# Another split of attention's steps over the blocks, and a quarter of the longest heads' differences on VectorE

## The chip, the cores and the metric

The kernel runs on one core of one Trainium2 chip. The metric is device time in microseconds. The kernel before was timed three times: 2462.47 us in the median, 2457.55 the lowest, 2462.65 the highest. Engines are named as in the profile: PE (TensorE), PEld (its weight loads), DVE (VectorE), ACT (ScalarE), POOL (GpSimd) and SP (SyncE, which only issues transfers).

## The reference

One layer on x of 2048 x 1024 in float32. A shared RMS norm and one projection feed three mixers: a gated convolution of width 3, a gated convolution of width 31 with a layer norm, and eight heads of stick-breaking attention. Their outputs are joined, projected by w_out and added to x; a squared-ReLU MLP of width 4096 and a last RMS norm follow. The attention is the part around the change:

```python
z = jnp.einsum("bhqd,bhkd->bhqk", qb, kb).astype(jnp.float32) * scale
mask = s_idx < t_idx
log_beta = jax.nn.log_sigmoid(z)
log_1m = jnp.where(mask, log_beta - z, 0.0)
suffix = lax.cumsum(log_1m, axis=3, reverse=True) - log_1m
a = jnp.where(mask, jnp.exp(log_beta + suffix), 0.0)
outs.append(jnp.einsum("bhqk,bhkd->bhqd", a.astype(v.dtype), vb))
```

The weight of a key is sigmoid(z) times the product of sigmoid(-z) over all later keys up to the query. The kernel computes with these products, not with logarithms.

## The kernel before, in words

All matrix products run in fp32r with each operand cut in two: hi is the operand rounded to fp32r by ACT (L88), lo is the rest, operand less hi, which `split` gives to DVE or POOL (L90). A product is then three matmuls, hi by hi, lo by hi and hi by lo (`mm3`, L103, L105, L107).

The sequence is cut into four blocks of 512 positions. A first stage computes the projections and mixers and the attention of block row 0. Then `block` runs four times, for tb = 0 to 3. Each run holds the output projection (ps_x, 192 matmuls), the scaling of the eight accumulators by ms (L961), and the MLP: 32 chunks of ffn1 (ps_u, 24 matmuls each, fl made by DVE at L915) and eight groups of ffn2 (ps_y, 96 matmuls each, added into acc by DVE at L940). In blocks 0 and 1 the raw MLP weights are also split and stored; later blocks load the split ones.

Attention for the block rows i = 1, 2, 3 is woven into blocks 0, 1 and 2. Row i needs its eight heads done by the end of block i - 1. A head has two passes of 3 + 4i steps each, three for the diagonal and 4i for full tiles of earlier keys:

- `a_pass1`: z = K by Q on PE (L513, L514), sigmoids on ACT (L591, L592), the running product R on DVE (L595), A times R on POOL (L593). At its end the products are carried across partitions by `a_cross_a` (a transpose, a scan at L609 and small products on DVE).
- `a_pass2`: A times the carried product on DVE (L651, for the diagonal L644), the split of A into Ahi (ACT) and Alo (POOL, line L90), then the product with V on PE (L697, L698, for the diagonal L689). Ahi and Alo have three buffers each.

KQd, the keys and queries of a head's own block, has one buffer. `a_load` issues its two transfers from POOL's queue once the head before has read it for the last time; the first z of the next head needs it. POOL's queue also issues the loads of Kl, Vd and Vl.

Pass 1 of one head runs with pass 2 of the head before it. Each step yields 0.5 units to `weave`, which advances attention while a block's own work, counted in costs, goes from 45 to 365 (320 in block 2); a full ffn1 chunk costs 5.2. The triple of numbers says how many units each block takes. A head of row i has 3.5 + 4i units: 60 for row 1, 92 for row 2, 124 for row 3, 276 together. What stands on each engine in which order is then settled by the scheduler of the tile framework, from the program's order and its own timeline.

Of the kernel before, what the change touches and what calls it, by code (L numbers as in the profile page):

```python
# [56 lines left out]
def weave(main, sides):  # L57

    done = 0.0
    sides = [(s, s.done, cost, t0, t1, last) for s, cost, t0, t1, last in sides]  # L60
    for c in main:
        done += c
        for s, base, cost, t0, t1, last in sides:
            s.advance(base + cost * min(max((done - t0) / (t1 - t0), 0.0), 1.0))
    for s, base, cost, t0, t1, last in sides:
        s.advance(float("inf") if last else base + cost)


class Trunk:
# [557 lines left out]
    def a_pass2(self, g):  # L627
        nc, pool, i, h, ab = self.nc, self.at, g["i"], g["h"], self.ab
        self.v_load(g)
        o = self.ps.tile([P, TB], F32, name="ps_o", tag="o", bufs=1)  # L630
        n = 3 + 4 * i
        Vl = None
        late = []
        for k in range(n):
            t = g["A0"][k]
            lo = pool.tile([P, TB], F32R, name="Alo", tag="Alo", bufs=self.ab["Alo"])
            hi = pool.tile([P, TB], F32R, name="Ahi", tag="Ahi", bufs=self.ab["Ahi"])
            if k in (0, 3):

                Q = self.ps.tile([P, TB], F32, name="ps_q", tag="q", bufs=1)  # L640
                nc.vector.transpose(Q, g["ql" if k else "qd"])
            if k < 3:
                qs = Q[:, 0:256] if k == 0 else Q[:, 256:512]
                nc.vector.tensor_tensor(  # L644
                    t.rearrange("p (a c) -> p a c", a=2),
                    t.rearrange("p (a c) -> p a c", a=2),
                    qs.unsqueeze(1).to_broadcast([P, 2, 256]),
                    op=ALU.mult,
                )
            else:  # L650
                nc.vector.tensor_tensor(t, t, Q, op=ALU.mult)  # L651
            self.split(hi, lo, t, "pool")
            v = None
            if k >= 3:
                j = 4 * i - 1 - (k - 3)
                if j % 4 == 3:
                    Vl = pool.tile([P, 4, P], F32R, name="Vl", tag="Vl", bufs=ab["Vl"])
                    vs = self.VS[h][0 : TB * i].rearrange("(p j) c -> p j c", j=4 * i)
                    self.load_r(Vl, vs[:, j - 3 : j + 1, :])
                v = Vl[:, j % 4, :]  # L660
            late.append((k, v, hi, lo))
            if len(late) > ab["late"]:
                self.a_av(g, o, n, *late.pop(0))
            yield 1
        for x in late:
            self.a_av(g, o, n, *x)
        tmp = pool.tile([P, TB], F32, name="otmp", tag="om", bufs=ab["om"])[:HD]
        nc.scalar.activation(tmp, o[HD:P], AF.Copy)

        if h % 2 == 0:  # L670
            self.yc = self.st.tile([P, TB], F32, name="yc", tag="y", bufs=self.ab["yc"])
        nc.vector.tensor_tensor(self.yc[HD * (h % 2) : HD * (h % 2) + HD], o[0:HD], tmp, op=ALU.add)
        if h == H - 1 and i:

            self.yraw[i, DC - 1] = self.yc
        elif h % 2:
            m = 4 + h // 2
            self.dma(self.Y[m * P : (m + 1) * P, i * TB : (i + 1) * TB], self.yc)
        self.heads[i] = self.heads.get(i, 0) + 1
        yield 0  # L680
# [330 lines left out]
    def build(self):  # L1011
        tc = self.tc
        with ExitStack() as ctx:
            self.consts(ctx)
            self.attention_consts(ctx)
            self.raw = ctx.enter_context(tc.tile_pool(name="raw", bufs=1))
            self.xb = 5
            self.presplit = [("w_out", c, q) for c in range(DC) for q in range(2)] + [("w1", c, q) for c in range(PRE) for q in range(2)]
            self.g, self.u, self.w, self.R, self.rv, self.sig, self.ca, self.ss, self.yraw = ({} for _ in range(9))
            with ExitStack() as c1:  # L1020
                self.psum_pool(c1, d=3, c=1, z=2, q=1, o=1)
                self.p_pools(c1)
                self.w_eng = "dve"
                self.sb = 2
                self.xl = [[None] * DC for _ in range(2)]
                self.xh = [[None] * DC for _ in range(2)]
                with tc.tile_pool(name="raw0", bufs=1) as self.rp:
                    self.rb, self.rt = 21, "raw"
                    self.p_start()
                self.rp = self.raw  # L1030
                self.rb, self.rt = self.xb, "xt"
                self.at = c1.enter_context(tc.tile_pool(name="at1", bufs=1))
                self.ab = dict(KQd=1, Kl=1, A0=5, om=2, Alo=2, Ahi=2, Vl=1, late=1, yc=2)
                weave(self.p_half(0), [(Side(self.mixer_b(0)), 83, 20, 225, True), (Side(self.x_norms()), 24, 60, 180, True)])
                self.heads = {}
                a0 = Side(self.attention([(h, 0) for h in range(H)]))
                weave(self.p_half(1), [(Side(self.mixer_b(1)), 98, 0, 200, True), (a0, 28, 0, 210, True), (Side(self.pre_split()), len(self.presplit), 0, 200, True)])
            with ExitStack() as c2:
                self.psum_pool(c2, d=3, z=3, q=1, o=1)
                self.at = c2.enter_context(tc.tile_pool(name="at2", bufs=1, reuse_waits="tile"))  # L1040
                self.st = c2.enter_context(tc.tile_pool(name="st2", bufs=1, reuse_waits="tile"))
                self.ha = c2.enter_context(tc.tile_pool(name="ha", bufs=1, reuse_waits="tile"))
                self.hp = c2.enter_context(tc.tile_pool(name="hp", bufs=1, reuse_waits="tile"))
                self.ob = 2
                self.kmax = 1536
                self.ab = dict(KQd=1, Kl=1, A0=15, om=2, Alo=3, Ahi=3, Vl=2, late=2, yc=1)
                at = Side(self.attention([(h, i) for i in (1, 2, 3) for h in range(H)]))
                self.heads = {}

                def attend(i):  # L1050
                    while self.heads.get(i, 0) < H:
                        at.advance(at.done + 1)

                self.attend = attend
                self.end = iter(())
                for tb in range(4):
                    weave(self.block(tb, self.end), [(at, (74, 95, 107)[tb], 45, 365 if tb < 2 else 320, False)] if tb < 3 else [])


_VECS = ["g_attn", "w_conv_a", "w_conv_b", "b_conv_b", "ln_b_g", "ln_b_b", "g_ffn", "g_final"]  # L1060
# [45 lines left out]
```

## Time and profile before

| what | value |
|---|---|
| median of three runs | 2462.47 us |
| the profiled execution | 2461.45 us |
| its span, first to last instruction | 2459.7 us |
| mean granted TensorE clock | 0.991 |
| busy: PE, DVE, ACT, POOL | 2397.3, 1629.8, 1032.8, 1139.2 us |
| POOL's differences Alo (L90) | 288, 399.1 us busy |

Block 0 stands from about 565 to 1065 us of the span, block 1 to 1563, block 2 to 2085, block 3 to the end. A row of a group reads: line, engine, operation, tiles out and in, shapes, count, then busy us and mean ns, then idle time before and what ended it. A row of the waits reads: who waited for whom, total us, times, longest us. A row of the timeline reads: start, duration, engine, line, what, how often, and in brackets the idle time before and what ended it. In the listings, SBUF tiles and PSUM tiles (those named ps_...) stand side by side; heads are counted from 0 in each row.

### The profile page before, as it was taken

How to read it: one execution, taken by the hardware profiler on the slowest of the kernel's cores; microseconds unless marked ns; L12 is line 12 of the kernel's file. 1: busy time of each engine (PE TensorE's matmuls, PEld its weight loads, DVE VectorE, ACT ScalarE, POOL GpSimd, SP SyncE). 2: the span in 40 equal slices, each digit the busy share in tenths (PEclk: the TensorE clock that was granted, in tenths of full speed). 3: DMA queues.
4: the chain of work that ended last, by engine and by line, in shares of the span. 5: the costliest groups of instructions: out<-in, count | busy, mean ns of one | idle time of the engine just before them, and what ended most of it. 6: DMA issues, size and time to landing. Idle time of an engine off the chain costs nothing.

```text
span 2459.7 us, 32438 instructions
## 1 busy us (share of the span) xinstructions
PE 2397.3 (97%) x11316; PEld 2016.1 (82%) x11316; DVE 1629.8 (66%) x2372; ACT 1032.8 (42%) x1910; POOL 1139.2 (46%) x1197
## 2 busy tenths in 40 slices
PE   8999989999999999999999999999999999999998
PEld 7888877898778878787878888888888888788887
DVE  7958599953898878867877768576666735212114
ACT  5232432232656656534555555345555532121121
POOL 0343256640667666515766677168887830000000
PEclk9999999999999999999999999999999999999999
DMA  7579897687688977787877777776666656655555
GB/s 260 190 257 311 285 301 202 210 276 234 180 223 236 243 217 196 184 275 242 250 221 246 228 227 204 264 222 186 187 204 189 199 180 201 240 196 184 202 188 189
DMA packets 236035, 549.04 MB, mean 223 GB/s; under 512 B 25696, under 2 KB 99424, under 8 KB 217440
## 3 DMA queue, kind: packets, MB, share of 16 engines
q1 hardware_dynamic: 179792, 472.50, 56.0%
q0 software_dynamic: 53888, 73.42, 15.8%
q8 instruction: 90, 1.47, 0.2%
q10 hardware_dynamic: 2192, 1.05, 0.2%
q14 instruction: 73, 0.60, 0.1%
HBM read 390.38 MB, written 148.11 MB: 219 GB/s over the span
## 4 chain that ended last, share of the span: by engine, by line
PE 72%; DVE 13%; DMA 9%; issue 3%; POOL 2%; ACT 1%; SPq 0%; POOLq 0%; DVEq 0%; ACTq 0%
PE ps_y L103 8%; PE ps_u L103 8%; PE ps_u L105 8%; PE ps_y L107 8%; PE ps_u L107 8%; PE ps_y L105 8%; PE ps_p L103 3%; PE ps_p L105 3%; PE ps_p L107 3%; DMA KQd<-KQ 2%; PE ps_z L513 2%; DVE ps_c L450 2%; PE ps_z L514 2%; PE ps_x L103 2%; PE ps_x L105 2%
## 5 line engine op out<-in xcount | busy, mean ns | idle before, releaser
L90 POOL TENSOR_TENSOR Alo<-A,Ahi 128x512 fp32r<-128x512 f32 x288 | 399.1, 1397 | 102.0 <-PE ps_o L698 43.8
L940 DVE TENSOR_TENSOR acc<-acc,ps_y 128x512 f32<-128x512 f32 (+1 forms) x264 | 174.7, 666 | 179.6 <-PE ps_y L107 178.3
L103 PE MATMUL ps_y<-fh,w 128*128 128x512 f32 (+1 forms) x1056 | 283.5, 386 | 8.4 <-DVE acc L940 4.7
L103 PE MATMUL ps_u<-hh,w 128*128 128x512 f32 x1024 | 279.5, 393 | 7.4 <-DMA w<-s_w 5.0
L107 PE MATMUL ps_y<-fl,w 128*128 128x512 f32 (+1 forms) x1056 | 278.6, 383 | 1.5 <-DVE fl L915 1.5
L105 PE MATMUL ps_y<-fh,w 128*128 128x512 f32 (+1 forms) x1056 | 279.5, 384 | 0.0
L593 POOL TENSOR_TENSOR A<-A,R 128x512 f32<-128x512 f32 x168 | 233.1, 1389 | 94.6 <-ACT A L591 70.7
L105 PE MATMUL ps_u<-hh,w 128*128 128x512 f32 x1024 | 276.9, 392 | 0.0
L107 PE MATMUL ps_u<-hl,w 128*128 128x512 f32 x1024 | 276.4, 390 | 0.0
L118 POOL TENSOR_TENSOR rs_y<-rs_v,mhalf 128x4 f32<-128x4 f32 (+1 forms) x13 | 14.5, 1115 | 546.1 <-DVE rs_v L117 486.0
L905 ACT ACTIVATE ps_u<-ps_u 128x512 f32<-128x512 f32 x128 | 74.7, 584 | 455.8 <-PE ps_u L107 455.8
L103 PEld LDWEIGHTS ps_y<-fh,w 128*128 128x128 f32 x1056 | 193.8, 189 | 47.9 <-DVE fl L915 4.5
L103 PEld LDWEIGHTS ps_u<-hh,w 128*128 128x128 f32 x1024 | 190.7, 189 | 47.5 <-DMA w<-s_w 7.2
L107 PEld LDWEIGHTS ps_y<-fl,w 128*128 128x128 f32 x1056 | 195.0, 188 | 41.4 <-DVE fl L915 2.5
L105 PEld LDWEIGHTS ps_y<-fh,w 128*128 128x128 f32 x1056 | 195.5, 189 | 39.8
L105 PEld LDWEIGHTS ps_u<-hh,w 128*128 128x128 f32 x1024 | 193.3, 189 | 41.4 <-DVE w L90 0.2
L107 PEld LDWEIGHTS ps_u<-hl,w 128*128 128x128 f32 x1024 | 192.4, 188 | 40.1
L915 DVE TENSOR_TENSOR fl<-ps_u,fh 128x512 fp32r<-128x512 f32 x128 | 87.5, 684 | 193.3 <-ACT fh L914 192.8
L595 DVE TENSOR_TENSOR R<-ps_z,R 128x512 f32<-128x512 f32 x168 | 115.4, 687 | 147.2 <-ACT ps_z L592 106.6
L88 ACT ACTIVATE Ahi<-A 128x512 fp32r<-128x512 f32 x288 | 177.2, 628 | 82.2 <-PE ps_o L697 35.9
L450 DVE SCALAR_TENSOR_TENSOR ps_c<-g,wb,ps_c 128x512 f32<-128x512 f32 x240 | 179.9, 750 | 4.7
L88 ACT ACTIVATE w<-wraw 128x512 fp32r<-128x512 f32 x152 | 91.9, 628 | 175.2 <-PE ps_y L107 113.1
(173 smaller groups left out, 4928.4 us busy)
## 6 DMA issues: line engine op xcount, KB each, us to landing
w<-s_w SPq DMA_DIRECT2D x200, 512.0 KB, 3.4
w<-s_w SPq DMA_DIRECT2D x68, 1024.0 KB, 4.8
wraw<-in_w SPq DMA_DIRECT2D x192, 256.0 KB, 4.7
w<-s_w_out SPq DMA_DIRECT2D x64, 512.0 KB, 5.0
s_w<-w SPq DMA_DIRECT2D x32, 1024.0 KB, 5.7
s_w<-w SPq DMA_DIRECT2D x56, 512.0 KB, 4.6
KQd<-KQ POOLq DMA_DIRECT2D x64, 384.0 KB, 6.9
xraw<-in_xT SPq DMA_DIRECT2D x48, 256.0 KB, 5.0
```

Source lines behind the costliest of these rows:

```text
L88: nc.scalar.activation(hi, x, AF.Copy)
L90: e.tensor_tensor(lo, x, f(hi), op=ALU.subtract)
L103: self.nc.tensor.matmul(ps, wh, xh, start=start and k == 0, stop=False)
L105: self.nc.tensor.matmul(ps, wl, xh, start=False, stop=False)
L107: self.nc.tensor.matmul(ps, wh, xl, start=False, stop=stop and k == n - 1)
L450: nc.vector.scalar_tensor_tensor(t, g[:, k : k + TB], self.wb[:, c, k : k + 1], t, op0=ALU.mult, op1=ALU.add)
L513: nc.tensor.matmul(z[:, oc], keys, g["qh"][:, qc], start=k == 0, stop=False)
L593: nc.gpsimd.tensor_tensor(t, t, R, op=ALU.mult)
L595: nc.vector.tensor_tensor(Rn, z, R, op=ALU.mult)
L905: nc.scalar.activation(ps, ps, AF.Relu)
L915: nc.vector.tensor_tensor(lo, ps, f(hi), op=ALU.subtract)
L940: nc.vector.tensor_tensor(acc[d][:, cols], acc[d][:, cols], ps, op=ALU.add)
```

## The change

Two edits. The units of attention per block become 66, 95 and 115, with the same sum. And in pass 2 of the heads of row 3 (15 tiles each), the lo part of tiles 3, 7 and 11 is computed by DVE, not POOL: 24 differences of 128x512.

```diff
-            self.split(hi, lo, t, "pool")
+
+            self.split(hi, lo, t, "dve" if i == 3 and k % 4 == 3 else "pool")
...
-                    weave(self.block(tb, self.end), [(at, (74, 95, 107)[tb], 45, 365 if tb < 2 else 320, False)] if tb < 3 else [])
+                    weave(self.block(tb, self.end), [(at, (66, 95, 115)[tb], 45, 365 if tb < 2 else 320, False)] if tb < 3 else [])
```

Behind the first edit all lines are one further down, so L915, L940, L961, L697 and L698 of before are L916, L941, L962, L698 and L699 of the change.

By the units, block 0 held all of row 1 and 14 units of row 2, and now holds 6 of row 2; block 1 ended 17 units into row 3, and now ends 9 units into it. The order of the rows on each engine follows. Three places:

The start of block 1 on DVE, where the eight accumulators are scaled by ms (acc). Before, the products of a head's full tiles with ps_q (A) stand ahead of them:

```order
L651 TENSOR_TENSOR A_10061<-A_10061,ps_q 128x512
L651 TENSOR_TENSOR A_10620<-A_10620,ps_q 128x512
L651 TENSOR_TENSOR A_10636<-A_10636,ps_q 128x512
L651 TENSOR_TENSOR A_10652<-A_10652,ps_q 128x512
L915 TENSOR_TENSOR fl<-ps_u,fh 128x512
L961 TENSOR_TENSOR acc_10301<-acc_10301,ms 128x512
L961 TENSOR_TENSOR acc_10311<-acc_10311,ms 128x512
```

And now, the same place:

```order
L644 TENSOR_TENSOR A_10453<-A_10453,ps_q 128x512
L644 TENSOR_TENSOR A_10473<-A_10473,ps_q 128x512
L644 TENSOR_TENSOR A_10498<-A_10498,ps_q 128x512
L916 TENSOR_TENSOR fl<-ps_u,fh 128x512
L673 TENSOR_TENSOR yc<-ps_o,otmp 64x512
L962 TENSOR_TENSOR acc_10128<-acc_10128,ms 128x512
L962 TENSOR_TENSOR acc_10138<-acc_10138,ms 128x512
```

Where the eight products of a head's full tiles stood (four of them shown), the three of a head's diagonal stand now; the eight of this head come some 30 rows further on.

Block 1 on PE, between the last z of head 6 of row 2 (ps_z from KQd and Kl) and the first z of head 7 (ps_z from KQd alone, 128x256). Before, from the last z on:

```order
L514 MATMUL ps_z<-KQd,Kl 128x512
L103 MATMUL ps_y<-fh,w_12881 128x512 x4
L105 MATMUL ps_y<-fh,w_12881 128x512 x4
L107 MATMUL ps_y<-fl,w_12881 128x512 x4
L697 MATMUL ps_o<-Ahi,Vl 128x512
L698 MATMUL ps_o<-Alo,Vl 128x512
L697 MATMUL ps_o<-Ahi,Vl 128x512
L698 MATMUL ps_o<-Alo,Vl 128x512
L103 MATMUL ps_y<-fh,w_13222 128x512 x4
L105 MATMUL ps_y<-fh,w_13222 128x512 x4
L107 MATMUL ps_y<-fl,w_13222 128x512 x4
```

Another twelve of ps_y and five of ps_u follow before head 7's first z. And now, up to that first z:

```order
L514 MATMUL ps_z<-KQd,Kl 128x512
L698 MATMUL ps_o<-Ahi,Vl 128x512
L699 MATMUL ps_o<-Alo,Vl 128x512
L698 MATMUL ps_o<-Ahi,Vl 128x512
L699 MATMUL ps_o<-Alo,Vl 128x512
L103 MATMUL ps_y<-fh,w_13127 128x512 x4
L105 MATMUL ps_y<-fh,w_13127 128x512 x4
L107 MATMUL ps_y<-fl,w_13127 128x512 x4
L103 MATMUL ps_y<-fh,w_13127 128x512 x4
L105 MATMUL ps_y<-fh,w_13127 128x512 x4
L107 MATMUL ps_y<-fl,w_13127 128x512 x4
L513 MATMUL ps_z<-KQd 128x256
```

The first z of the head moved from 45 matmuls behind the last z of the head before to 28.

Block 2 on DVE, behind the twelve products of a head of row 3. Before:

```order
L651 TENSOR_TENSOR A_15562<-A_15562,ps_q 128x512
L651 TENSOR_TENSOR A_15615<-A_15615,ps_q 128x512
L915 TENSOR_TENSOR fl<-ps_u,fh 128x512
L940 TENSOR_TENSOR acc_15113<-acc_15113,ps_y 128x512
L557 TENSOR_TENSOR Rd<-om 128x256
L566 TENSOR_TENSOR R<-om 128x256
```

And now, of the same kind of place:

```order
L651 TENSOR_TENSOR A_15678<-A_15678,ps_q 128x512
L651 TENSOR_TENSOR A_15708<-A_15708,ps_q 128x512
L941 TENSOR_TENSOR acc_15142<-acc_15142,ps_y 128x512
L90 TENSOR_TENSOR Alo<-A_15334,Ahi 128x512
L941 TENSOR_TENSOR acc_15181<-acc_15181,ps_y 128x512
L557 TENSOR_TENSOR Rd<-om 128x256
```

The first of the head's three differences (Alo) came in between two additions into acc; the other two stand some 10 and 23 rows further on.

## The prediction

> **What bounds the kernel now.** I read the page first, then the time by block, then PE's waits in each block, and last the rows around the longest waits.
>
> ```profile
> PE 2397.3 (97%) x11316; PEld 2016.1 (82%) x11316; DVE 1629.8 (66%) x2372; ACT 1032.8 (42%) x1910; POOL 1139.2 (46%) x1197
> PE   8999989999999999999999999999999999999998
> POOL 0343256640667666515766677168887830000000
> ```
>
> PE is busy for 97% of the span, and the change removes no matmul. So only PE's idle time and its half-clock time can be won. POOL works until slice 32 of 40 and not after: that is attention's stretch. The four blocks by their stretches (PE, PEld, DVE, ACT, POOL busy, then granted clock, DMA share, GB/s):
>
> ```profile
> 565.00:1065.00 500.00, 486.70 (x2251) 405.43 (x2250) 388.44 (x543) 272.21 (x509) 286.88 (x325) 0.99 0.77 213
> 1065.00:1563.00 498.00, 488.11 (x2220) 408.55 (x2219) 378.82 (x540) 254.50 (x475) 298.00 (x309) 1.00 0.78 237
> 1563.00:2085.00 522.00, 517.74 (x2342) 435.10 (x2341) 331.46 (x481) 244.71 (x447) 317.09 (x310) 1.00 0.67 203
> 2085.00:2459.70 374.70, 364.25 (x1710) 305.15 (x1708) 91.15 (x156) 67.35 (x119) 1.39 (x2) 0.99 0.57 201
> ```
>
> PE misses 13.3 us in block 0 (500.00 less 486.70), 9.9 in block 1, and 4.3 in block 2, which has the most attention. Block 0 has the least attention and loses most: DVE is busy there for 388 of 500 us, because it also splits raw weights. What PE waited for, block 0, then block 1, then block 2:
>
> ```profile
> PE ps_z L513 <- DMA KQd<-KQ: 4.9, 3, 2.4
> PE ps_y L103 <- DVE acc L940: 4.1, 3, 2.5
> PE ps_u L103 <- DVE acc L940: 2.3, 1, 2.3
> PE ps_y L103 <- DVE fl L915: 1.3, 1, 1.3
> PE ps_y L107 <- DVE fl L915: 0.5, 1, 0.5
> ...
> PE ps_z L513 <- DMA KQd<-KQ: 4.7, 2, 3.6
> PE ps_u L103 <- DMA w<-s_w: 2.4, 2, 1.7
> PE ps_o L698 <- POOL Alo L90: 0.9, 1, 0.9
> ...
> PE ps_y L103 <- DVE fl L915: 2.3, 1, 2.3
> PE ps_u L103 <- DMA w<-s_w: 0.9, 1, 0.9
> ```
>
> In block 0 it is half the load of the next head's keys and queries (KQd, one buffer, issued from POOL once the last z has read it), and half DVE being late with the main chain. POOL itself holds PE for 0.9 us in all. The longest wait on KQd is in block 1:
>
> ```profile
> 1218.47 0.39 PE L514 MATMUL ps_z<-KQd,Kl 128*128 128x512 f32 x1
> 1218.70 1.09 PE L103 MATMUL ps_u<-hh,w 128*128 128x512 f32 x4
> 1219.17 1.36 POOL L83 DMA_DIRECT2D KQd<-KQ  x2 [2.00 <-PE ps_z L514]
> 1234.33 0.36 PE L513 MATMUL ps_z<-KQd 128*128 128x256 f32 x1 [3.63 <-DMA KQd<-KQ]
> 1236.18 1.91 PE L103 MATMUL ps_u<-hh,w 128*128 128x512 f32 x4
> 1235.00:1238.40 3.40, 3.40 (x15) 2.92 (x14) 1.05 (x2) 3.32 (x7) 2.56 (x5) 0.55 1.04 274
> ```
>
> A stall of this size costs more than itself: the granted clock after it was 0.55 for 3.4 us, and four matmuls took 1.91 us instead of 1.09. I count 1.7 us more for such a stall (half of 3.4, an estimate).
>
> **The change part by part.** The profiled execution took 2461.45 us (span 2459.7 and 1.75 around it), 1.0 below the median of 2462.47. The sum below is made against 2461.45, and the time forecast is the median plus the sum. Up to about 630 us and behind the last head of attention the rows of all engines stand as before, so only the 1360 us between count.
>
> *Eight units leave block 0, and eight enter block 2.* A head of block row i has 3.5 + 4i units, so the three rows have 60, 92 and 124 units, 276 in all, like both triples. PE's total does not move. DVE's waits in block 0 (4.1 + 2.3 + 1.3 + 0.5 = 8.2 us) meet 66 units in place of 74: by proportion 0.9 us less. DVE is near its limit there, and a queue grows faster than its load, so I take 3.0. Bounds: nothing, and all 8.2. Block 2 takes the eight units at its own price, 4.3 us lost on 107 units: 0.3 us more.
>
> *The start of block 1.* This is the place where the order changes most to the good. Before, a head of row 2 ends its first pass just there, its eight rests are multiplied ahead of the main chain, and the next head's loads start among the weights':
>
> ```profile
> 1110.69 4.26 DVE L651 TENSOR_TENSOR A<-A,ps_q 128x512 f32<-128x512 f32 x7
> 1115.48 13.30 DVE L961 TENSOR_TENSOR acc<-acc,ms 128x512 f32<-128x512 f32 x8
> PE ps_z L513 <- DMA KQd<-KQ: 1.1, 1, 1.1
> ```
>
> The last row is of PE's waits from 1095 to 1130 us; the 2.4 on weights and the 0.9 on Alo quoted above for block 1 fall in the same 35 us, 4.4 us in all. Now the first pass of that head only begins at the start of the block: its three products for the diagonal are all that stands ahead of the eight scalings, and the next KQd load, which follows its last z, comes 129 main matmuls later (after 336 of the block's, not 207). I take all of the 4.4 us as won; bounds nothing, since the waits on weights may come from SP's queue alone, and 4.4.
>
> *The distance from the last z of a head to the first of the next.* The load needs 0.7 us until its first issue (1218.47 to 1219.17), 0.7 for the second (half of 1.36), and then its landing. Landings of KQd in blocks 0, 1 and 2:
>
> ```profile
> DMA to landing us min/median/max: 4.5/7.4/11.3
> DMA to landing us min/median/max: 5.0/8.0/17.1
> DMA to landing us min/median/max: 4.5/5.9/7.5
> ```
>
> So a head needs 8.8, 9.4 and 7.3 us at the median. Against that I counted the matmuls of PE's order between the two, at 0.2265 us for 512 columns (1.81 us for eight):
>
> ```profile
> 49.26 1.81 PE ps_p L103 x8
> 51.08 1.81 PE ps_p L105 x8
> ```
>
> In block 0 the seven loads within row 1 had 9.5 to 11.8 us and now have 9.5 to 14.5; the two tightest stay. I take no gain there, with 4.9 us as the bound. In block 1 the heads 3 and 4 of row 2 (counted from 0) now have 14.9 and 12.7 us where they had 10.6 and 11.8. The stall at 1234 us came from a slow landing with 11.8 us of cover; I take three quarters of its 3.6 + 1.7, that is 4.0, as gone, between nothing and 5.3, because another load may be the slow one. Against it stands head 7 of row 2: its first z comes 24 main matmuls and four of attention after the last z (6.3 us), where it had 41 and four (10.2 us). It needs 9.4, so PE stands for 3.1 us, with half the clock loss (0.85): 3.9 us lost. Bounds: 0 (a landing of 5.0) and 12.5 (17.1, and the clock). Heads 1 and 5 of row 3 shrink to 8.6 us (in block 1) and 6.9 (in block 2): 0.8 and 0.4 us short at the median, and as the first had 10.0 without a wait I count half of its 0.8, so 0.8 us lost for the two; bounds 0, and 1.2 more by the longest landing of block 2 (7.5).
>
> *Twenty-four rests on VectorE.* Three of the twelve differences (A less its rounded half) of each of the eight longest heads leave POOL for DVE. The nearest rows, all of them groups:
>
> ```profile
> L90 POOL TENSOR_TENSOR Alo<-A,Ahi 128x512 fp32r<-128x512 f32 x97 | 129.3, 1340 | 46.7 <-PE ps_o L698 37.3 <-PE ps_o L697 6.5 <-ACT Ahi L88 2.4
> L90 DVE TENSOR_TENSOR w<-wraw,w 128x512 fp32r<-128x512 f32 x152 | 148.0, 993 | 24.0 <-ACT w L88 23.4
> L915 DVE TENSOR_TENSOR fl<-ps_u,fh 128x512 fp32r<-128x512 f32 x128 | 87.5, 684 | 193.3 <-ACT fh L914 192.8
> 1691.02 7.26 DVE L651 TENSOR_TENSOR A<-A,ps_q 128x512 f32<-128x512 f32 x12
> DVE R L595 <- ACT ps_z L592: 60.6, 21, 6.2
> DVE R L595 <- POOL A L593: 16.8, 16, 2.0
> ```
>
> POOL is spared 24 x 1.34 = 32 us. That wins nothing by itself: in block 2 POOL's differences waited 43.8 us for PE (37.3 + 6.5) to free their buffers, not the other way round, and no KQd wait of PE stands in block 2's rows. DVE gets 24 instructions. The same subtraction of two SBUF tiles took 993 ns on DVE in the mean, against 684 where one operand lies in PSUM. So it is 24 us of DVE's 522, which had 190 free. The danger is its place. DVE works in order, the difference waits for ACT's Ahi, and behind it stand acc and fl, on which PE waits. The first difference of a head comes right behind twelve products in a row (7.26 us). One of those convoys already cost PE the 2.3 us on fl at 1697, and 0.85 of clock. But DVE's head also stood up to 6.2 us for R in this block, 21 times on ACT, and PE lost nothing by it. I take half of one more stall like that at 1697: 1.5 us lost. Bounds: 2 won, if the spared POOL keeps DVE's scans from waiting, and eight such stalls, 25 us lost.
>
> A rule speaks against this edit. The Trainium skill, "SBUF — State Buffer", section "Who interferes with whom", says that a DVE instruction with two SBUF inputs contends with a GpSimd instruction that reads SBUF, and that the second to start fully blocks. The 993 ns beside 684 agree with it. By the rule a difference that starts just behind one of POOL's waits its whole length, which is the slower rival below.
>
> Sum: -3.0 + 0.3 - 4.4 - 4.0 + 3.9 + 0.8 + 1.5 = -4.9 us, and I round to -5. From 2461.45 that is 2456.5 for an execution like the profiled one, and from the median **2457.4 us**, 0.2% faster: at the edge of what a measurement of this kernel tells from no change, which I set at 0.2% (4.9 us).
>
> **The rivals.** *The stalls only change places.* For it: each of the long stalls hangs on one slow landing or one convoy, and with another order other heads meet them; the terms of the sum are of both signs and cancel. Against it: block 0's DVE is spared in any order. Then the terms on single stalls (-4.4, -4.0, 3.9, 0.8) are nothing in sum, and block 0 keeps only its proportional 0.9: 2462.
>
> *The rests hold VectorE up (slower).* One mechanism: a difference behind the twelve products meets POOL at work and stands up to 1.34 us more, 0.69 + 1.34 = 2.03 us, on top of 7.26, and acc and fl come late for PE. It decides once DVE is held for longer than about two ps_y tiles of twelve matmuls, 5.4 us. For it: the 2.3 us at 1697, and the 4.26 + 13.30 us rows above, where DVE's scalings of two SBUF tiles took 1.66 us each. Against it: seven of eight convoys cost nothing before. If four heads in place of half a one stall for 2.3 + 0.85, that is 12.6 us in place of 1.5: the sum turns from -4.9 to +6.2, so 2468.6. The skill's rule named above would bring just this.
>
> *Everything loosens (clearly faster).* DVE's 8.2 us of block 0 go whole and head 7's load lands within 5 us: another 5.2 + 3.9 = 9.1 off, 2448. For it: DVE falls behind in bursts, not evenly. Against it: the weight splitting of block 0 stays.
>
> **How the numbers follow.** The forecast has 0.47, with its own range of 2451 to 2461; I give 0.34 of that to over 0.2% faster and 0.13 to within. Stalls that only move have 0.26: 0.03 faster, 0.17 same, 0.06 slower. The rests in VectorE's way have 0.19, slower. The loosening has 0.08, faster. So faster 0.45, same 0.30, slower 0.25. The range takes in the two outer cases nearly whole, since the bounds of head 7's load and of the rests are wide upwards: 2447 to 2470.
>
> **What would show it.** Right: block 0's PE waits on acc and fl under 6 us in sum; no wait of PE on weights or Alo in the first 65 us of block 1; a wait on KQd of some 3 us at head 7 of row 2; DVE's Alo differences at about 1 us each, and PE's waits on DVE in block 2 under 5 us. Wrong: Alo differences near 2 us with PE waiting on acc or fl behind them (the second rival); KQd waits of 3 us or more at heads that I gave cover; block 2 losing more than block 0 gains.

## The result, and the profile after

The changed kernel takes 2480.35 us in the median of six runs (2477.53 to 2481.55), the one before 2462.56 (2457.55 to 2464.68). The ratio is 1.0082, with a 95% interval of 1.0065 to 1.0098: 17.8 us slower, where 5 us faster was forecast, and outside the forecast's range. The profiled execution took 2478.15 us, its span is 2476.4, 16.7 more than before.

Blocks 0, 1 and 2 of the changed kernel by their stretches (columns as in the prediction):

```profile
560.00:1055.00 495.00, 488.69 (x2274) 407.97 (x2274) 365.06 (x528) 267.61 (x501) 270.21 (x313) 1.00 0.79 220
1055.00:1566.00 511.00, 488.73 (x2184) 407.72 (x2183) 379.03 (x535) 249.63 (x466) 290.41 (x304) 0.98 0.74 227
1566.00:2101.00 535.00, 524.07 (x2365) 438.65 (x2364) 367.30 (x525) 252.68 (x465) 304.28 (x304) 1.00 0.65 197
```

PE misses 6.3 us in block 0 (13.3 before), but 22.3 in block 1 (9.9) and 10.9 in block 2 (4.3). The loss sits in block 1, and from there on. What PE waited for in the changed kernel, in block 0, in block 1 from 1240 us on, and in block 2:

```profile
PE ps_y L103 <- DVE acc L941: 3.6, 3, 2.8
PE ps_z L513 <- DMA KQd<-KQ: 1.7, 2, 1.3
...
PE ps_u L103 <- DMA w<-s_w: 6.7, 4, 4.0
PE ps_y L103 <- DVE acc L941: 4.5, 3, 3.1
PE ps_x L103 <- DVE acc L941: 3.7, 1, 3.7
PE ps_o L690 <- DVE yc L673: 2.7, 1, 2.7
PE ps_z L513 <- DMA KQd<-KQ: 1.8, 1, 1.8
...
PE ps_z L513 <- DVE R L595: 3.1, 3, 1.7
PE ps_x L103 <- DMA w<-s_w_out: 2.7, 2, 1.9
PE ps_y L103 <- DVE fl L916: 1.9, 1, 1.9
```

To compare kernels place by place, I count PE's lost time between equal numbers of matmuls of the main chain (ps_x, ps_u and ps_y, 1728 in a block): of each distance between the starts of two matmuls, what lies above the streaming time of the first (0.2262 us for 512 columns). Half-clock time is in it.

| lost by PE, us | before | after |
|---|---|---|
| block 0 | 24.9 | 15.4 |
| block 1, up to its matmul 1008 | 19.2 | 14.2 |
| block 1, 1008 to 1440 ("late block 1") | 2.1 | 13.0 |
| block 1 from 1440, block 2 to 288 ("the boundary") | 7.1 | 24.1 |
| rest of block 2 | 11.5 | 18.1 |
| first 290 of block 3 | 4.8 | 5.3 |
| sum | 69.6 | 90.1 |

Of the 20.5 us in the sum, 3.7 go off because block 0 began that much earlier in this execution (565.1 us, not 568.8), though nothing differs ahead of it. The two gains are there: 9.5 and 5.0 us. Late block 1 takes 10.9, the boundary 17.0.

In what follows, the row of eight or twelve products with ps_q (L651) that follows a head's first pass is called its burst, and a VectorE instruction is called held when it lasts longer beside GpSimd's work than the same instruction alone.

**Late block 1.** Rows of DVE, POOL, SP's queue and PE of the changed kernel, in order of time:

```profile
1353.32 4.87 DVE L651 TENSOR_TENSOR A<-A,ps_q 128x512 f32<-128x512 f32 x8
1363.62 1.49 POOL L90 TENSOR_TENSOR Alo<-A,Ahi 128x512 fp32r<-128x512 f32 x1
1363.86 4.91 DVE L90 TENSOR_TENSOR w<-wraw,w 128x512 fp32r<-128x512 f32 x2
1365.66 1.31 POOL L90 TENSOR_TENSOR Alo<-A,Ahi 128x512 fp32r<-128x512 f32 x1
1366.92 1.29 POOL L593 TENSOR_TENSOR A<-A,R 128x512 f32<-128x512 f32 x1
1369.69 0.87 SPq L79 DMA_DIRECT2D w<-s_w  x1
1376.55 2.77 DVE L90 TENSOR_TENSOR w<-wraw,w 128x512 fp32r<-128x512 f32 x2
1377.63 0.33 SPq L79 DMA_DIRECT2D wraw<-in_w  x1
1379.35 0.33 SPq L79 DMA_DIRECT2D s_w<-w  x1
1380.24 11.77 SPq L79 DMA_DIRECT2D w<-s_w  x5
1386.38 2.08 PE L103 MATMUL ps_u<-hh,w 128*128 128x512 f32 x4 [4.03 <-DMA w<-s_w]
```

Two differences of raw weights take 4.91 us while POOL works through differences and products; the pair at 1359.25 us took 1.28. The next two take 2.77. SP issues one transfer after the other: a raw load waits for one of these differences (7.0 us), the store of the split piece follows it, so from 1370.56 (1369.69 + 0.87) to 1380.24 us no load of ready weights goes out, and PE stands 4.03 us for one of those issued then. The holds are some 5 us of this (4.91 and 2.77 less twice 1.28); for the rest VectorE works through other rows without a gap, the burst at 1353 us (4.87 us) among them. That the burst put the differences behind is read from this order of the rows.

**The boundary.** Here head 0 of row 3 ends its first pass, and y for block 2 is split:

```profile
1515.65 8.49 DVE L90 TENSOR_TENSOR yl<-yraw,yh 128x512 fp32r<-128x512 f32 x1
1516.08 1.33 POOL L90 TENSOR_TENSOR Alo<-A,Ahi 128x512 fp32r<-128x512 f32 x1
1517.34 1.31 POOL L593 TENSOR_TENSOR A<-A,R 128x512 f32<-128x512 f32 x1
1518.59 2.56 POOL L90 TENSOR_TENSOR Alo<-A,Ahi 128x512 fp32r<-128x512 f32 x2
1521.11 1.26 POOL L593 TENSOR_TENSOR A<-A,R 128x512 f32<-128x512 f32 x1
1522.34 1.25 POOL L90 TENSOR_TENSOR Alo<-A,Ahi 128x512 fp32r<-128x512 f32 x1
1524.06 1.27 DVE L941 TENSOR_TENSOR acc<-acc,ps_y 128x512 f32<-128x512 f32 x2
1524.79 2.08 PE L103 MATMUL ps_y<-fh,w 128*128 128x512 f32 x4 [3.06 <-DVE acc L941]
...
1539.57 5.46 DVE L651 TENSOR_TENSOR A<-A,ps_q 128x512 f32<-128x512 f32 x9
1544.95 3.45 DVE L801 TENSOR_TENSOR ss<-ss,sq 128x512 f32<-128x512 f32 x1
1545.34 2.52 POOL L90 TENSOR_TENSOR Alo<-A,Ahi 128x512 fp32r<-128x512 f32 x2
1548.33 1.27 DVE L651 TENSOR_TENSOR A<-A,ps_q 128x512 f32<-128x512 f32 x2
1549.52 0.68 DVE L941 TENSOR_TENSOR acc<-acc,ps_y 128x512 f32<-128x512 f32 x1
1550.25 1.19 PE L103 MATMUL ps_x<-y,w 128*128 128x512 f32 x4 [3.70 <-DVE acc L941]
```

One subtraction is held for 8.49 us, through six POOL instructions, and the two acc behind it are what PE waits for. Then nine products, a held ss and two more products stand ahead of an acc of block 1, and PE's ps_x waits for it. Before, the same burst came at 1503 us, 43.5 us ahead of block 2's first ps_x (1 us ahead of it now), and the long hold there fell on a weight difference; PE's only wait from 1525 to 1563 us was 0.5 us on acc:

```profile
1503.02 4.27 DVE L651 TENSOR_TENSOR A<-A,ps_q 128x512 f32<-128x512 f32 x7
...
1530.92 5.26 DVE L90 TENSOR_TENSOR w<-wraw,w 128x512 fp32r<-128x512 f32 x1 [0.27 <-ACT w L88]
```

### The profile page after: what moved, and what is told of

It is laid out like the page before. It is cut to its first block, busy times and chain, and to the rows that moved or that the text cites. A ratio compares the mean times of both kernels' runs of the same rounds, so it can differ in the third digit from the quotient of the medians.

```text
span 2476.4 us, 32439 instructions
## 1 busy us (share of the span) xinstructions
PE 2402.0 (97%) x11316; PEld 2018.3 (82%) x11316; DVE 1641.1 (66%) x2396; ACT 1031.9 (42%) x1910; POOL 1101.0 (44%) x1173
## 3 DMA queue, kind: packets, MB, share of 16 engines
q0 software_dynamic: 53888, 73.42, 15.7%
## 5 line engine op out<-in xcount | busy, mean ns | idle before, releaser
L90 POOL TENSOR_TENSOR Alo<-A,Ahi 128x512 fp32r<-128x512 f32 x264 | 362.4, 1382 | 87.8 <-PE ps_o L699 33.8
L941 DVE TENSOR_TENSOR acc<-acc,ps_y 128x512 f32<-128x512 f32 (+1 forms) x264 | 174.6, 664 | 150.3 <-PE ps_y L107 148.7
L103 PEld LDWEIGHTS ps_y<-fh,w 128*128 128x128 f32 x1056 | 192.8, 189 | 48.9 <-DVE acc L941 10.8
L916 DVE TENSOR_TENSOR fl<-ps_u,fh 128x512 fp32r<-128x512 f32 x128 | 87.8, 686 | 207.4 <-ACT fh L915 207.1
L90 DVE TENSOR_TENSOR w<-wraw,w 128x512 fp32r<-128x512 f32 x152 | 150.5, 1008 | 32.3 <-ACT w L88 31.3
```

Source lines behind the costliest of these rows:

```text
L90: e.tensor_tensor(lo, x, f(hi), op=ALU.subtract)
L103: self.nc.tensor.matmul(ps, wh, xh, start=start and k == 0, stop=False)
L916: nc.vector.tensor_tensor(lo, ps, f(hi), op=ALU.subtract)
L941: nc.vector.tensor_tensor(acc[d][:, cols], acc[d][:, cols], ps, op=ALU.add)
```

## The experiments

All edits are against the kernel before; the diffs show parts of the lines only. "Late" and "boundary" are PE's lost time in the stretches defined above, from one profiled execution each. Executions of one kernel differ by 10 to 20 us (2455.39 to 2467.78 in ten of `units_66_92`, 2448.43 to 2470.16 in twenty of the kernel before), so a difference of 2 or 3 us in a stretch says little. In block 0 even 5 us say little: the six kernels with PE's order of before there (before itself among them) lost 24.2 to 30.7 us, the nine with the change's order 15.4 to 20.7. The profiled execution of `even_66_103` took 9.8 us less than its median, that of `units_66_92` 7.2 less, that of `store_all_66_103` 8.2 more.

| kernel | block 0 | block 1 to 1008 | late | boundary | rest of block 2 | median | ratio, 95% interval |
|---|---|---|---|---|---|---|---|
| rests_only | 26.2 | 17.8 | 2.8 | 5.6 | 16.7 | 2463.57 | 1.0005 to 1.0043 |
| units_only | 16.5 | 17.6 | 14.2 | 25.1 | 11.7 | 2478.28 | 1.0039 to 1.0090 |
| units_66_103 | 17.3 | 20.1 | 17.5 | 7.8 | 11.2 | 2463.50 | 0.9988 to 1.0026 |
| units_74_87 | 30.7 | 17.5 | 3.6 | 23.4 | 12.3 | 2479.11 | 1.0049 to 1.0102 |
| units_70 | 31.5 | 17.2 | 11.5 | 11.7 | 13.6 | 2480.49 | 1.0057 to 1.0101 |
| end_345 | 18.1 | 20.6 | 13.5 | 14.9 | 12.1 | 2472.18 | 1.0031 to 1.0063 |
| store_act | 17.8 | 18.7 | 9.7 | 19.2 | 12.0 | 2469.40 | 1.0026 to 1.0070 |
| rests_half | 28.0 | 21.1 | 2.1 | 5.3 | 17.3 | 2464.94 | 1.0007 to 1.0038 |
| store_74 | 24.2 | 26.9 | 2.8 | 6.7 | 8.9 | 2463.97 | 1.0000 to 1.0028 |
| store_66_103 | 17.5 | 26.1 | 15.7 | 7.2 | 10.6 | 2468.58 | 1.0018 to 1.0047 |
| store_345 | 17.6 | 27.2 | 18.3 | 16.7 | 12.3 | 2483.87 | 1.0059 to 1.0111 |
| store_all_66_103 | 25.0 | 24.9 | 16.4 | 7.8 | 10.5 | 2473.16 | 1.0034 to 1.0074 |
| early_66_95 | 20.7 | 23.8 | 6.1 | 17.2 | 12.1 | 2467.85 | 1.0014 to 1.0041 |
| early_74_95 | 27.6 | 30.2 | 3.0 | 10.6 | 12.3 | 2477.80 | 1.0054 to 1.0094 |
| units_66_92 | 18.8 | 11.9 | 7.3 | 17.1 | 13.0 | 2462.57 | 0.9996 to 1.0025 |
| even_66_103 | 20.7 | 22.7 | 2.4 | 16.2 | 9.2 | 2472.85 | 1.0030 to 1.0065 |
| quiet_74 | 14.7 | 20.4 | 2.9 | 5.9 | 6.0 | 2439.96 | 0.9892 to 0.9930 |
| quiet_66 | 10.8 | 8.6 | 3.7 | 11.9 | 7.2 | 2430.49 | 0.9867 to 0.9897 |

### The change taken apart

`units_only` has the units without the rests, `rests_only` the rests without the units:

```diff
- (74, 95, 107)[tb]
+ (66, 95, 115)[tb]          # units_only
- self.split(hi, lo, t, "pool")
+ self.split(hi, lo, t, "dve" if i == 3 and k % 4 == 3 else "pool")   # rests_only
```

> Only the units become 66, 95, 115; all differences of the longest heads stay on POOL. PE's order up to the end of block 1 is that of the change. Theory U (the move of eight units brings the loss: row 2's later heads now meet block 1's weight splitting on DVE, whose stores hold SP's queue and so the weight loads): the second half of block 1 loses some 20 us against before as in the change, and the time is 2474 to 2481. Rival R (the differences on DVE hold it up): block 0 keeps its gain, blocks 1 and 2 lose nothing, and the time is 2450 to 2460.

> Only the 24 differences go to DVE; units stay 74, 95, 107. Theory U: within 4 us of before, 2459 to 2467. Rival R: block 2 alone loses 12 us or more, 2472 to 2482, with PE waiting on acc, fl or R behind DVE's Alo rows.

`units_only` takes 2478.28 us, 17.5 above the 2460.76 that before took beside it (1.0064). That is nearly the whole loss; it keeps block 0's gain (16.5) and has the same two lossy stretches. `rests_only` is 1.0024 times before, some 3 to 6 us in the profile and the medians. The units are the cause of most of it. Then each half of the move alone: `(66, 103, 107)` gives block 0's eight units to block 1, `(74, 87, 115)` gives block 1's to block 2.

> Units 66, 103, 107, no differences on DVE: block 0 has PE's order of the change, block 2 that of before, and block 1 takes the eight units. Theory U: block 0 gains 10 us of waits as in the change, block 1 with eight units more beside its weight splitting gives back that much or more: 2460 to 2475. Rival R: no loss anywhere but the block 1 share, 2452 to 2460.

> Units 74, 87, 115, no differences on DVE: block 0 has the order of before, block 2 that of the change, and block 1 has eight units less. Theory U: block 1 is lighter and loses less than before, block 2 with POOL unrelieved loses a few us: 2452 to 2463. Rival R: the same without the last loss, 2450 to 2458. If block 2's order itself (115 units) is what costs, 2468 to 2476.

The two halves part the two losses cleanly. With 66 units in block 0, late block 1 loses 17.5 us and the boundary 7.8; with 115 in block 2, late block 1 loses 3.6 and the boundary 23.4. In the total the second half costs about as much as the whole (1.0076), and the first nothing that can be measured (1.0007). The table explains that only in part: block 0 loses 7.6 us less, and this profiled execution took 4.2 us more than its median.

### First theories

`units_70` is `(70, 95, 111)`. `end_345` spreads block 1's attention until cost 345 (the change's units). `store_act` issues block 1's stores of split w2 from ACT's queue, so that SP's loads don't stand behind them (the change's units). `rests_half` has before's units and doubles the rests on VectorE, six of twelve.

```diff
- 365 if tb < 2 else 320
+ (365, 345, 320)[tb]        # end_345
- self.dma(self.split_w[name][at], t)
+ if tb == 1:                # store_act
+     self.nc.scalar.dma_start(self.split_w[name][at], f(t))
+ else:
+     self.dma(self.split_w[name][at], t)
- self.split(hi, lo, t, "pool")
+ self.split(hi, lo, t, "dve" if i == 3 and k > 2 and k % 2 else "pool")   # rests_half
```

> Units 70, 95, 111, no differences on DVE. Theory B (what costs is where a head's burst of products on DVE falls: the first head of row 3 has its burst after 159.5 units, the second of row 2 after 77, and a burst within about two units of a block's end or just behind its start meets the y splits and the last additions into acc): the blocks end at 70 and 165 units, clear of every burst, so no loss at either boundary, 2450 to 2462. Rival M (block 2 can't take more units): half of the loss of 115, 2467 to 2473.

> Units 66, 95, 115, no differences on DVE, but block 1's 95 units are done by cost 345, not 365, so that the burst of the first head of row 3 falls some 20 us ahead of the block's end. Theory B: from matmul 1440 of block 1 to 288 of block 2 PE loses 12 us or less, where the units alone lost 25 and before 7; 2462 to 2470. Rival M (block 2 can't take more units): 2475 to 2482, with the loss in the same place or inside block 2.

> Units 66, 95, 115, no differences on DVE, and the stores of the split w2 pieces of block 1 go out from ACT's queue, not SP's. Theory W (from matmul 1008 to 1296 of block 1 the weight loads stand in SP's queue behind such stores and raw loads, which wait for DVE's splits): PE's waits on weights there, 7.3 us with the units alone, fall to 2 or less and the time by 5 to 11 us, to 2468 to 2474. Rival (the loads wait for their buffers or for the raw loads alone): waits and time stay, 2475 to 2481; the boundary loss stays in both.

> Units 74, 95, 107 as before; six of the twelve differences of the longest heads on DVE, 48 in all, not 24. Rule L (a DVE instruction with two SBUF inputs stands while POOL reads SBUF): the differences take 1.3 us or more in the mean and the cost of rests_only doubles: 2466 to 2474. Rival (DVE has room): 2460 to 2465.

`units_70` is a miss in the total (2480.49): the boundary did fall to 11.7, but late block 1 lost 11.5, and block 0, at 31.5, shows nothing of the gain, so half the move keeps much of the price and not the gain. `store_act` came out at 2469.40, the time expected, but PE's waits on weights from matmul 1008 to 1296 only halved (6.0 to 3.0 us), where I had expected 2 or less. `end_345` took 2472.18, some 2 us above what I had given it, and its boundary fell to 14.9, not to 12 or less. Twice as many rests cost no more than once: 1.0023 beside 1.0024.

### Do the two cures add up?

`store_74` and `store_66_103` are the stores' edit with units 74, 95, 107 and 66, 103, 107; `store_345` joins it with end 345; `store_all_66_103` sends the stores of block 0 by ACT too.

```diff
- if tb == 1:
+ if True:                   # store_all_66_103, beside store_act's edit
```

> The units of before (74, 95, 107); only the stores of split w2 pieces in block 1 go out on ACT's queue. Theory W+E (the loss is two things: loads of w1 that stand in SP's queue behind such stores late in block 1, and a head's burst at the end of block 1): before lost only 1.5 us in matmuls 1008 to 1296 of block 1, so there is next to nothing to win: 2456 to 2463, and that stretch keeps 1 to 3 us. Rival C (every order has collisions of its own, and any edit deals them anew): the total may lie 5 us or more to either side, by losses in stretches that the store does not touch.

> Units 66, 103, 107, and the stores on ACT's queue. That order without the stores' edit took 2463.5 us: 7.6 us won in block 0, 16.2 lost in matmuls 1008 to 1296 of block 1 against 1.5 before. Theory W+E: the edit halves the 16.2, as it did with 66, 95, 115 (12.4 to 6.3), and leaves the rest: 2463.5 less 8 is 2455.5, range 2452 to 2459, faster than before. Rival C: the stretch improves but others get worse by as much: 2460 or more.

> Units 66, 95, 115, the stores on ACT's queue, and block 1's attention spread until cost 345 in place of 365. Theory W+E: the two edits won 8.9 and 6.1 us one by one and act on different stretches, so together 15: 2478.3 less 15 is 2463, range 2460 to 2467. Rival C (both only dealt the stalls anew): no better than the better of the two, 2469 or more.

> Units 66, 103, 107, and all stores of split weights on ACT's queue, those of w_out and w1 in block 0 too. Theory W: SP's loads in block 0 no longer stand behind stores; block 0's waits on weights are small, so 0 to 2 us less than with the stores of block 1 alone: 2452 to 2458. Rival: ACT works in order too, and an issue that waits for DVE's difference holds up the rounded halves fh, hh and w behind it; block 0 loses 5 us or more: 2460 or more.

`store_74` came out 1 us above its range, at 2463.97, with late block 1 as expected. In the other three the expectation failed. Late block 1 stayed at 15.7 with 66, 103, 107 (17.5 without the edit), and the two cures together gave 2483.87, more than either alone. `store_all_66_103` lost 25.0 us in block 0 against 17.5 in `store_66_103`, as its rival had said, but PE's waits that grew there were those on KQd (11.3 us against 1.6). The stores are a link of the chain and not its cause. SP's waits in late block 1, of `units_66_103` first, then of `store_66_103`:

```profile
SPq L79 <- PE ps_u L107: 28.9, 10, 5.3
SPq L79 <- DVE w L90: 23.5, 9, 8.9
```

```profile
SPq L79 <- PE ps_u L107: 33.2, 10, 5.6
SPq L79 <- DVE w L90: 25.8, 9, 7.4
```

With the stores gone from SP, it stands as long for DVE's differences: the raw loads need the buffers that these free.

### Number of units, or place of the bursts?

A head of row 2 takes some 180 main matmuls at 95 units (172 to 188 between its bursts in `units_only`), a ps_u and a ps_y stretch together 192, so the bursts of eight products keep nearly one place against them. Of the bursts of eight in block 1, six of seven fell in ps_u stretches before, and six of seven in ps_y stretches in `units_only`. Four kernels move the bursts apart from the units:

```diff
- (74, 95, 107)[tb], 45, 365 if tb < 2 else 320
+ (66, 95, 115)[tb], 23 if tb == 1 else 45, (365, 343, 320)[tb]   # early_66_95
+ (74, 95, 107)[tb], 23 if tb == 1 else 45, (365, 343, 320)[tb]   # early_74_95
+ (66, 92, 118)[tb], 45, 365 if tb < 2 else 320                   # units_66_92
+ (66, 103, 107)[tb], 0 if tb == 1 else 45, (365, 394, 320)[tb]   # even_66_103
```

> The change's units (66, 95, 115, no rests on VectorE), but block 1 spreads its attention from cost 23 to 343, not 45 to 365: the same pace, half a ps_u and ps_y pair earlier. Theory P (a head's burst of eight products on VectorE costs PE 3 to 9 us when it falls in a ps_y stretch of block 1, about 1 in a ps_u stretch; and the burst of head 0 of row 3 must lie 25 us or more ahead of the boundary): the bursts of heads 2 to 7 fall in ps_u stretches (first products behind matmul 504, 692, 864, 1044, 1224, 1392), that of row 3 at 1608. Matmuls 1008 to 1296 lose at most 4 us (12.4 in units_only), the boundary at most 13 (25.1): 2478.3 less 8 less 12 is 2458, range 2453 to 2465. Rival U (the numbers of units are the cause): 2472 to 2482. Rival C (each order has collisions of its own): the losses come back elsewhere, 2467 or more.

> The units of before (74, 95, 107), block 1 from cost 23 to 343. Theory P: the bursts of row 2 move from ps_u stretches (seven of eight) to ps_y stretches (first products behind 372, 552, 720, 900, 1091, 1272), so matmuls 1008 to 1296 lose 6 to 12 us in place of 1.5, and the stretches ahead of them lose too; the boundary stays at about 7: 2468, range 2464 to 2475. Rival U: no unit leaves its block, so nothing is lost there: 2457 to 2463. Rival C: any total, without a loss in the ps_y stretches.

> Units 66, 92, 118. Three more units go from block 1 to block 2, and the burst of row 3's head 0 falls behind the boundary, once block 2's attention has started. Theory P (boundary part): the boundary loses 13 us or less in place of 25; the row 2 bursts stay in ps_y stretches, so late block 1 still loses 8 to 16: 2478.3 less 12 is 2466, range 2460 to 2472. Rival M (block 2 can't take the units; the loss at the boundary grows with their number): the boundary loses 25 or more, 2478 to 2490.

> Units 66, 103, 107, block 1's attention spread from cost 0 to 394, so that a head of row 2 takes about as long as a ps_u and a ps_y stretch together (some 205 main matmuls against 192) and its bursts stay in or near ps_u stretches (first products behind 432, 648, 852, 1056, 1268, 1464); row 3's head 0 is at 1668, nearer to the boundary than before's 1584. Theory P: block 0 keeps its gain of 8 us, late block 1 loses at most 5 (16.3 with the steeper window), the boundary 10 to 15: 2463.5 less 11 plus 5 is 2457, range 2452 to 2463. Rival C: 2463 or more. Rival X: attention ahead of cost 45 meets the split of y and w_out's loads at the start of block 1: 5 us or more lost in its first 192 matmuls.

`early_74_95` moves no unit out of its block and costs 17.4 us (2477.80). `units_66_92` puts three units more than the change into block 2 and costs nothing that can be measured. So the numbers of units alone are not the cause; what the order brings together is. But the rule on places held only in part: only `units_66_92` came out within its range, and its boundary lost 17.1 us, not 13 or less. `early_74_95` lost ahead of matmul 1008 (30.2), not behind it as I had expected, and there on weights. PE's longest wait in sum there, from 990 to 1357 us; before had 2.4 us on these weights up to the same matmul:

```profile
PE ps_u L103 <- DMA w<-s_w: 10.6, 4, 3.8
```

`early_66_95` brought late block 1 down to 6.1 but lost 20.7 and 23.8 ahead of it; `even_66_103` has late block 1 at 2.4, loses 22.7 ahead of it, and took 2472.85. Over the 18 kernels with POOL's differences (before and after among them), PE lost 2.2 us in the 144 main matmuls behind a burst that fell in a ps_u stretch of block 1 (65 of them between matmuls 380 and 1540, mean), and 3.3 behind one in a ps_y stretch (51), with up to 8.7 in both. Drawing the edges of the stretches a little otherwise gives 2.6 (62 bursts) and 3.1 (54). That is at most a tendency, not a rule to plan by.

### What holds VectorE

The last two kernels take away what the rows above show at each place: POOL's differences. ScalarE writes the lo tiles of attention with a scaled copy in their place. Left out is thus the exact rest of A, and the output isn't the reference's; VectorE and PE keep their instructions, in a somewhat other order: across the boundary, PE is 3 attention matmuls in the mean (12 at most) ahead of or behind its place in `units_only`. ScalarE has 288 copies more.

```diff
+ if eng == "act":
+     nc.scalar.activation(lo, x, AF.Copy, scale=2.0**-12)
+     return
...
- self.split(hi, lo, t, "pool")
+ self.split(hi, lo, t, "act")
```

> Units 66, 95, 115. Left out: the 264 + 24 exact differences Alo of attention on GpSimd; in their place ScalarE writes the same tiles with a scaled copy (so the output is not the reference's), and VectorE and PE keep their instructions. GpSimd keeps the masks, the products L593 and its DMA issues. Theory S (GpSimd's back-to-back work on SBUF holds VectorE's two-SBUF subtractions, and PE waits behind them): no subtraction of VectorE takes over 4 us, matmuls 1008 to 1296 of block 1 lose at most 5 us (12.4 in units_only) and the boundary at most 12 (25.1); 2455 to 2465, and at most 6 us more than quiet_74. Rival V (VectorE's own bursts at these places are the cause): the boundary still loses 18 or more, and quiet_66 is 12 us or more above quiet_74. Rival A: ScalarE, with 288 copies of 0.6 us more, becomes late for PE; both kernels lose alike.

> Units 74, 95, 107 with the same differences of GpSimd replaced by scaled copies on ScalarE (output not the reference's). Theory S: VectorE's subtractions shrink to about 0.7 us each; as before lost only 7 us at the boundary and 1.5 late in block 1, there is little to win there, 2448 to 2462. Rival A (ScalarE becomes late): 2465 or more.

Both are far faster than I had expected, and the sign of the change turns: with POOL's differences gone, the change's units take 2430.49 us (2428.43 to 2434.28) and before's 2439.96 (2433.33 to 2440.84), 9.5 us less in place of 17.5 more. VectorE's differences by their groups, of `units_only` first, then of `quiet_66` (its lines stand three further down):

```profile
L90 DVE TENSOR_TENSOR w<-wraw,w 128x512 fp32r<-128x512 f32 x152 | 150.7, 1009 | 33.6 <-ACT w L88 32.7
L651 DVE TENSOR_TENSOR A<-A,ps_q 128x512 f32<-128x512 f32 x192 | 117.5, 678 | 0.5
L90 DVE TENSOR_TENSOR yl<-yraw,yh 128x512 fp32r<-128x512 f32 x5 | 15.5, 3107 | 0.0
```

```profile
L93 DVE TENSOR_TENSOR w<-wraw,w 128x512 fp32r<-128x512 f32 x152 | 115.9, 776 | 47.5 <-ACT w L88 46.8
L93 DVE TENSOR_TENSOR yl<-yraw,yh 128x512 fp32r<-128x512 f32 x5 | 6.5, 1320 | 0.0
```

And PE's waits across the boundary, of `units_only` (1459 to 1640 us) and then of `quiet_66` (1424 to 1593):

```profile
PE ps_y L103 <- DVE acc L940: 4.7, 2, 3.1
PE ps_x L103 <- DVE acc L940: 4.5, 1, 4.5
```

```profile
PE ps_u L106 <- DMA w<-s_w: 2.7, 3, 1.4
PE ps_x L106 <- DMA w<-s_w_out: 1.3, 1, 1.3
PE ps_x L106 <- DVE acc L943: 0.5, 1, 0.5
```

Late block 1 loses 3.7 in place of 14.2, the boundary 11.9 in place of 25.1. The bursts did not move away: the seven of eight products in block 1 begin within 13 main matmuls of their places in `units_only`. Behind the one at matmul 1135 of the block (1127 in `quiet_66`), the next 144 main matmuls lost 7.0 us in `units_only` and 0.8 in `quiet_66`. POOL's differences are most of what makes these places dear. What the pair does not part: it spares POOL some 380 us (1128.7 busy in `units_only`, 749.3 in `quiet_66`), so POOL's own lateness goes with VectorE's holding. In blocks 0 to 2 of `units_only` PE waited for no Alo at all, which speaks for the holding. About a third of the boundary's price stays (11.9 against 5.9 in `quiet_74`), and its cause is open: of PE's waits there, 4.0 us are on weights and 0.5 on acc.

No kernel with the whole computation was faster than the one before; the nearest are `units_66_103` at 1.0007 (0.9988 to 1.0026) and `units_66_92` at 1.0010 (0.9996 to 1.0025).

## Why the prediction was wrong, step by step

- **"Block 2 takes the eight units at its own price ... 0.3 us more"** is the step that failed, and with it the choice to work out only the start of block 1. A block has no price per unit: the units shift every later head against the main chain. The boundary cost 17.0 us and late block 1 10.9, for which the sum had only this 0.3 and the 3.9 for head 7's wait. I looked at the place that the order changed "most to the good" and not at where block 1 would now end, 9 units into row 3. The first pass of its head 0 ends at 7.5 of them, so its burst had to fall near the boundary.
- **Block 0's DVE waits, −3.0 (bounds nothing and 8.2).** Right: they fell by 3.6 us, from 8.2 to 4.6 (3.6 on acc, 1.0 on yc), and the sign to look for, waits on acc and fl under 6 us, is there. But block 0 gained 9.5 us in all (8.4 and 7.6 in `units_only` and `units_66_103`). Another 3.2 are waits on KQd (4.9 to 1.7), for which I had taken no gain; the rest lies in no wait that the view lists.
- **The start of block 1 (−4.4) and the slow KQd landing of row 2's head 4 (−4.0), against head 7 (+3.9).** The stretch up to matmul 1008 gained 5.0 of the 8.4 us, but `units_only`, with the same order of PE in block 1, gained only 1.6, so how much of it was really won is open. The burst ahead of the scalings is gone, and so is the KQd wait there, but a wait of 2.3 us on w_out stands 34 us behind block 1's first ps_x, in the 65 us that I had called free of waits on weights. Head 7 did wait, where it was said, 1.8 us and not 3.1:

```profile
1063.94 2.05 PE L103 MATMUL ps_x<-y,w 128*128 128x512 f32 x4 [2.31 <-DMA w<-s_w_out]
1407.63 0.36 PE L513 MATMUL ps_z<-KQd 128*128 128x256 f32 x1 [1.77 <-DMA KQd<-KQ]
```

- **The 24 rests, +1.5 (bounds −2 and 25).** Too small: 3 to 6 us by `rests_only` against its own before. The rest of block 2 lost 16.7 there and 18.1 in the change, against 11.5 before and 11.7 in `units_only`, and PE's waits on DVE in block 2 are 5.2 us (3.1, 1.9 and 0.2 on acc), where I had set 5. A rest took 1.46 us in the mean, between the 1 us that I took for harmless and the 2 of the slower rival; twice as many, in `rests_half`, cost no more and took 1.11 each.

```profile
L90 DVE TENSOR_TENSOR Alo<-A,Ahi 128x512 fp32r<-128x512 f32 x24 | 35.1, 1461 | 11.5 <-ACT Ahi L88 8.6 <-PE ps_o L699 2.5 <-PE ps_o L698 0.2
```

- **The slower rival named the right mechanism at the wrong instructions.** It had VectorE's two-SBUF instructions held by POOL, and the rule cited from the Trainium skill ("SBUF — State Buffer", section "Who interferes with whom") for it. It applied them to the 24 rests alone. The same rule bears on every weight difference, every yl and every ss, and at the boundary two of these, held for 8.49 and 3.45 us, stand ahead of what PE waited for. The trace of `units_only` agrees with the rule in which instructions are held: the product with ps_q, with one operand in PSUM, took 678 ns over 192 instructions, the weight differences 1009 over 152.
- **"The stalls only change places"** is what happened, except that the sum was not nothing.
- The forecast of each single stall hung on before's stalls. The sum could take these away one by one, but the new order brought stalls of its own, and the range counted only those at places that I had looked at. The signs to look for had the same gap: none of them lies at the end of block 1.

## What to carry to other kernels

When a number moves woven work along a main chain, price the new places, above all what now falls on the end of each block, and not only the stalls that go. On each engine look for the instructions that another engine can hold, and ask of each which in-order queue or accumulator stands behind it. Where a shift's gain is eaten like this, the remedy may lie with the holder: here the same shift lost 17.5 us beside GpSimd's differences and won 9.5 without them.

## What was not expected of the hardware

A held VectorE instruction did not get its turn when one GpSimd instruction ended: the difference at 1515.65 us stood 8.49 us through six of them, back to back, and ended 0.5 us behind the last (at 1524.14, the last at 1523.59). So the price of a hold can be the length of GpSimd's unbroken run, not one instruction of 1.3 us. It is not always the whole run: the differences at 1007.22 us (4.93 long) and 1470.62 (7.51) got their turn inside one, and GpSimd's next instruction then took 1.72 us. And the holding in itself grew little: 19 VectorE operations on two tensors (TENSOR_TENSOR) took over 2 us in blocks 0 to 2 before, the scans not counted, 49 us above 0.69 each in sum, against 15 and 54 after, or 17 and 63 with the two hl (SCALAR_TENSOR_TENSOR) that took so long only after. By the rows shown, what decides is what stands behind the held one; no run tests this by itself.
